# Splitting a sample group's expert pass over two blocks and keeping both halves of the trunk's weights in HBM, in a one-core decoder step

## The chip, the cores and the metric

One core of one Trainium2 chip runs the whole step as one program. The metric is the device time of that program in microseconds (us), the median of several executions. Engines are TensorE (PE in the profile, with PEld for its weight loads), VectorE (DVE), ScalarE (ACT), GpSimd (POOL) and SyncE (SP), which issues most DMAs. A DMA that the program issues from POOL stands in POOL's queue.

## The reference, cut to what matters

One decoder layer over 1024 prompt rows and 64 sample rows, width 1024:

```python
z = rmsnorm(x) @ w_in                       # lru_x | lru_gate | q | k | v | gate_lru | gate_attn
A = rglru(conv(lru_x)) * gelu(lru_gate)     # -> @ w_branch_lru
B = window_attention(q, k, v)               # 128-wide window, ALiBi, sinks -> @ w_branch_attn
merged = sigmoid(gate_lru) * (A @ w_branch_lru) + sigmoid(gate_attn) * (B @ w_branch_attn)
h = x + merged @ w_out
y = h + peer(rmsnorm(h))
# peer: 8 heads x 16 experts for each row, out of 16384, by product keys:
act = gelu(x_row . expert_u[idx]) * g       # 128 experts a row
out = sum(act * expert_v[idx])
```

## The kernel before

The rows pass through the trunk (everything up to `h` and the top-k scores) in three blocks: block 0 has 256 prompt rows and the 64 sample rows, blocks 1 and 2 have 384 prompt rows each. A last stage, `dense`, follows: it walks all 16384 experts for the prompt rows of blocks 0 and 1 and gathers single experts for those of block 2.

**Stages of a block**, in the order in which the code is written (`trunk`): attention; eight steps of gate and attention projection, merged into `mg` (L322 is the eviction); the recurrent branch (`lru`); eight steps of gate and recurrent projection (L337); `w_out` in four column groups (L356); the second norm, whose transposes are L267; and `retrieve`, 16 groups of query projection and top-k.

**Weights.** Matmuls take each float32 operand as a high and a low part (`hi`, `lo`), so that each product is three matmuls (L183 to L185). A weight comes in chunks of 512 KB; there are 84 chunks a block. Block 0 loads a chunk (`wraw`), makes the high part on ACT and the low part on DVE (`split`, L163 and L164), and POOL's queue writes the low part to `lo_d` in HBM (L212). Blocks 1 and 2 load the raw chunk and the low part, and make the high part again on ACT (L208). There are three buffers each for `wraw`, `whi` and `wlo`. The raw chunk is a strided slice of the weight matrix, in runs of 512 or 1024 bytes; `lo_d` lies in runs of 4096 bytes.

**Work behind a block.** What belongs to a block's experts is done while the next block's trunk runs: `behind(b)` is a generator, and `bg(k)` in the trunk advances it by k steps. The tables `PG1` (during block 1) and `PG2` (during block 2) give k for each stage: merge steps, recurrent groups, second merge, `w_out` groups, norm tiles, retrieve groups, q/k/v groups of the attention, score groups. The steps are, in this order:

- `choose(b)`: the top 16 expert pairs of each row, on DVE.
- For block 0 alone, the sample rows' experts: `early_u` gathers 64 slices of `expert_u` (each gather brings 512 KB: 128 rows of 4 KB) by a DMA that POOL issues (L961), and DVE reduces each (L963); `early_v` does the same with `expert_v` (L976, L981) and writes the sample rows' result to `out_y` (L988). Both hold the tile `et`, with three row slots inside it. Two of these go with each step.
- `build_g(b)`: for each group of four rows, one-hot tiles on DVE (`oij`; L939 to L941), four matmuls into a PSUM tile of the tag `tr` (L922), and a copy on ACT into `sg` (L923); a "product" below is one such group. After eight products `sg` goes to HBM (`g_d`, L925). Block 0 has 64 products, block 1 has 96.

**Buffers that are shared.** `et`, `sg` and the attention's keys and values all use the one buffer of the tag `at`: a `sg` can't be written before `et` is done with. The three PSUM tiles of the tag `tr` go round among the products, the norm's transposes and the retrieval, in the order in which the code asks for them.

**Order.** A scheduler puts each engine's instructions into one fixed order when the program is built; an engine then takes them one by one, and waits where the next is not ready.

**Scores** (`scores`): for each block of 128 queries and each key head, four matmuls with 64 contracted rows, two for heads on partitions 0 to 63 and then two for heads on partitions 64 to 127, each pair with its PSUM tile (L460), and four evictions on DVE (L463).

## Time and profile before

| what | value |
|---|---|
| median of 3 runs | 3769.24 us (3755.25 to 3769.95) |
| the profiled execution | 3754.26 us |
| its span, first to last instruction | 3752.5 us |
| PE busy | 3336.7 us, 89% |
| DVE busy | 2882.6 us, 77% |
| POOL busy | 1520.3 us, 41% |
| ACT busy | 1268.9 us, 34% |
| DMA | 1012.37 MB, mean 270 GB/s |

The span begins with the first instruction and ends with the last; times inside it are given from its start. Block 0 ends near 470 us, block 1 near 1235 us, block 2 near 1795 us, and `dense` takes the rest. The profile has a strip of 40 slices (one is 93.8 us) that shows how busy each engine was, and a table of who waited for whom; a wait that an engine spends on something that is not late costs nothing, so a wait counts only where the engine that waits has no other work and the work after it is late too.

### The profile page before, as it was taken

What the parts mean: (1) busy time and instruction counts of PE and PEld (TensorE: products, weight loads), DVE (VectorE), ACT (ScalarE), POOL (GpSimd) and SP (SyncE); (2) the same over time, 40 slices, a digit from 0 to 9 for tenths busy, and PEclk for the clock granted to TensorE, in tenths of its full rate; (3) what the DMA queues carried; (4) which work ended last, traced back from release to release, by engine and by line L of the source; (5) the groups of instructions that cost most, each with busy time, mean ns of one, the idle gap of its engine ahead of it and who ended that gap; (6) DMA issues with size and microseconds to landing.
All of it is one profiled execution on the core that took longest, in us unless ns stands there. A gap on an engine that the chain in (4) does not pass through costs nothing.

```text
span 3752.5 us, 58800 instructions
## 1 busy us (share of the span) xinstructions
PE 3336.7 (89%) x21891; PEld 3211.5 (86%) x21891; DVE 2882.6 (77%) x6803; ACT 1268.9 (34%) x2331; POOL 1520.3 (41%) x1240
## 2 busy tenths in 40 slices
PE   6899999883058989999889999999999999999996
PEld 6798988883058869998779999999999999999996
DVE  5567797984577988867899787777777776777777
ACT  4555454641033455743222222222222222222221
POOL 0011100223400000000367677677767776777774
PEclk8899999987579999999889999999999999999998
DMA  7388856998747627788488989989989888999988
GB/s 230 99 268 282 284 169 194 326 310 309 234 147 266 199 86 245 247 288 280 160 276 300 310 314 317 314 306 320 320 306 312 308 307 305 318 326 313 306 307 284
DMA packets 551327, 1012.37 MB, mean 270 GB/s; under 512 B 39452, under 2 KB 357852, under 8 KB 547936
## 3 DMA queue, kind: packets, MB, share of 16 engines
q1 hardware_dynamic: 409920, 494.75, 40.9%
q0 software_dynamic: 141120, 513.86, 38.5%
q8 instruction: 172, 2.82, 0.3%
q14 instruction: 115, 0.94, 0.1%
HBM read 904.14 MB, written 105.99 MB: 269 GB/s over the span
## 4 chain that ended last, share of the span: by engine, by line
PE 28%; DMA 18%; DVE 13%; issue 8%; POOL 7%; ACT 2%; SPq 0%; POOLq 0%; DVEq 0%; ACTq 0%
DMA row<-in_expert_v,iA 6%; DMA row<-in_expert_u,iA 4%; PE tr L922 3%; DMA et<-in_expert_v,est 3%; PE ou L183 3%; PE ou L184 3%; PE ou L185 3%; PE mm L185 3%; PE mm L183 3%; PE mm L184 3%; PE sc L183 3%; PE sc L184 3%; PE sc L185 3%; POOL row L888 2%; DVE row L890 2%
## 5 line engine op out<-in xcount | busy, mean ns | idle before, releaser
L183 PE MATMUL ou<-ah,vh 128*128 128x384 f32 (+1 forms) x2048 | 634.0, 314 | 42.5 <-ACT ah L163 20.2
L183 PE MATMUL sc<-dx,uh 128*128 128x256 f32 (+1 forms) x2048 | 637.7, 311 | 19.7 <-DVE al L164 10.3
L185 PE MATMUL sc<-dx,ul 128*128 128x256 f32 (+1 forms) x2048 | 635.9, 311 | 1.0 <-POOL ul L164 1.0
L184 PE MATMUL sc<-dx,uh 128*128 128x256 f32 (+1 forms) x2048 | 636.5, 311 | 0.0
L184 PE MATMUL ou<-al,vh 128*128 128x384 f32 (+1 forms) x2048 | 630.5, 310 | 1.9 <-DVE al L164 1.9
L185 PE MATMUL ou<-ah,vl 128*128 128x384 f32 (+1 forms) x2048 | 629.4, 310 | 0.5 <-POOL vl L164 0.5
L164 POOL TENSOR_TENSOR ul<-un,uh 128x1024 fp32r<-128x1024 f32 x128 | 308.2, 2408 | 790.3 <-ACT uh L163 787.4
L902 DVE SCALAR_TENSOR_TENSOR acc<-row,hv,acc 128x1024 f32<-128x1024 f32 x384 | 493.1, 1284 | 127.5 <-DMA row<-in_expert_v,iA 124.3
L890 DVE SCALAR_TENSOR_TENSOR row<-row,xt 128x1024 f32<-128x1024 f32 x384 | 465.0, 1216 | 138.7 <-DMA row<-in_expert_u,iA 136.5
L900 POOL DMA_INDIRECT row<-in_expert_v,iA x384 | 361.6, 942 | 278.6 <-DVE acc L902 202.9
L888 POOL DMA_INDIRECT row<-in_expert_u,iA x384 | 365.8, 953 | 265.5 <-DVE row L890 186.4
L183 PEld LDWEIGHTS ou<-ah,vh 128*128 128x128 f32 x2048 | 385.6, 190 | 59.8 <-DVE dac L1077 27.1
L183 PEld LDWEIGHTS sc<-dx,uh 128*128 128x128 f32 x2048 | 392.5, 192 | 21.4 <-DVE al L164 11.7
L185 PEld LDWEIGHTS sc<-dx,ul 128*128 128x128 f32 x2048 | 391.9, 191 | 1.5 <-POOL ul L164 1.5
L184 PEld LDWEIGHTS sc<-dx,uh 128*128 128x128 f32 x2048 | 392.3, 192 | 0.0
L184 PEld LDWEIGHTS ou<-al,vh 128*128 128x128 f32 x2048 | 388.1, 190 | 3.6 <-DVE al L164 2.7
L185 PEld LDWEIGHTS ou<-ah,vl 128*128 128x128 f32 x2048 | 387.6, 190 | 0.7 <-POOL vl L164 0.7
L922 PE MATMUL tr<-oij 128*128 128x128 f32 x1280 | 169.3, 288 | 202.4 <-ACT sg L923 200.7
L1077 DVE TENSOR_TENSOR dac<-dac,ou 128x384 f32<-128x384 f32 (+1 forms) x672 | 313.8, 481 | 38.2 <-PE ou L185 37.2
L922 PEld LDWEIGHTS tr<-oij 128*128 128x128 f32 x1280 | 164.6, 204 | 206.9 <-ACT sg L923 202.2
L164 POOL TENSOR_TENSOR vl<-vn,vh 128x1024 fp32r<-128x1024 f32 x128 | 309.2, 2420 | 14.6 <-ACT vh L163 12.6
L163 ACT CAST uh<-un 128x1024 fp32r<-128x1024 f32 x128 | 134.4, 1050 | 459.7 <-PE sc L184 360.9
(295 smaller groups left out, 7357.0 us busy)
## 6 DMA issues: line engine op xcount, KB each, us to landing
wlo<-lo_d SPq DMA_DIRECT2D x168, 512.0 KB, 4.9
wraw<-in_w_in SPq DMA_DIRECT2D x132, 512.0 KB, 5.9
un<-in_expert_uT SPq DMA_DIRECT2D x128, 512.0 KB, 5.9
vn<-in_expert_v SPq DMA_DIRECT2D x128, 512.0 KB, 5.8
lo_d<-wlo POOLq DMA_DIRECT2D x84, 512.0 KB, 6.0
g_d<-sg SPq DMA_DIRECT2D x20, 2048.0 KB, 6.9
wraw<-in_peer_w_query SPq DMA_DIRECT2D x48, 512.0 KB, 6.2
gt<-g_d SPq DMA_DIRECT2D x32, 768.0 KB, 10.3
```

Source lines behind the costliest of these rows:

```text
L163: nc.scalar.copy(hi, src)
L164: return (lo_eng or nc.vector).tensor_tensor(lo, src, f32(hi), op=ALU.subtract)
L183: nc.tensor.matmul(ps, lh, rh, start=first and j == 0, stop=False)
L184: nc.tensor.matmul(ps, lh, rl, start=False, stop=False)
L185: nc.tensor.matmul(ps, ll, rh, start=False, stop=last and j == n - 1)
L888: nc.gpsimd.indirect_dma_start(out=row, out_offset=None, in_=i["expert_u"], in_offset=bass.IndirectOffsetOnAxis(ap=ia[:, s:s + 1], axis=0))
L890: nc.vector.scalar_tensor_tensor(row, row, 1.0, xt, op0=ALU.mult, op1=ALU.mult, accum_out=hv[:, s:s + 1])
L900: nc.gpsimd.indirect_dma_start(out=row, out_offset=None, in_=i["expert_v"], in_offset=bass.IndirectOffsetOnAxis(ap=ia[:, s:s + 1], axis=0))
L902: nc.vector.scalar_tensor_tensor(acc, row, hv[:, s:s + 1], acc, op0=ALU.mult, op1=ALU.add)
L922: nc.tensor.matmul(pt[:, x, :], oj[:, x], wi[:, x], start=True, stop=True)
L1077: nc.vector.tensor_tensor(ac[k // 4][:, k % 4, a:b], ac[k // 4][:, k % 4, a:b], ps[:, 0:b - a], op=ALU.add)
```

## The change

- `wsplit`, `load_c` and `load_n` become `weights`: the first block that loads a chunk writes both halves to HBM from POOL's queue (`hi_d` and `lo_d`); the later blocks load both halves and neither load the raw chunk nor copy on ACT.
- `behind`: block 0's generator has `early_u` alone, block 1's generator has `early_v`; one gather goes with a step, no longer two. `early_v` starts in block 2 when the attention has given up the tag `at`.
- `scores`: both PSUM tiles are asked for first, and the four matmuls alternate between the two halves of the partitions; the four evictions follow.
- `PG1` and `PG2` have new numbers.

```diff
-PG1 = (6, 5, 4, 5, 2, 2, 0, 0)
-PG2 = (5, 5, 4, 3, 2, 2, 2, 1)
+PG1 = (5, 5, 4, 5, 2, 2, 0, 0)
+PG2 = (6, 6, 5, 1, 2, 4, 2, 2)
...
-    def wsplit(self, key, hi, lo, raw):
...
-        if use > 1:
-            nc.scalar.copy(hi, raw)
-            nc.sync.dma_start(f32(lo), kept)
-            return
-        self.split(hi, lo, raw)
-        nc.gpsimd.dma_start(kept, f32(lo))
+    def weights(self, src, r0, c0, nk, nc_):
...
+        if first:
+            raw = sp.tile([P, nk, nc_], F32, tag="wraw", name="wraw", bufs=NR)
+            self.wdma = nc.sync.dma_start(raw, src.rearrange("(k p) c -> p k c", p=P)[:, r0:r0 + nk, c0:c0 + nc_])
+            self.split(hi, lo, raw)
+            nc.gpsimd.dma_start(kept[0], f32(hi))
+            nc.gpsimd.dma_start(kept[1], f32(lo))
+        else:
+            nc.sync.dma_start(f32(hi), kept[0])
+            self.wdma = nc.sync.dma_start(f32(lo), kept[1])
...
-            for par in range(2):
...
+            pss = [self.mm().rearrange("p (g s) -> p g s", s=256) for _ in range(2)]
+            for g in range(4):
+                pr = slice(g % 2 * HD, g % 2 * HD + HD)
+                nc.tensor.matmul(pss[g % 2][:, g // 2, 0:S], qT[pr, 2 * j + g // 2, :], kT[pr, j, c0 + b0:c0 + 2 * P], start=True, stop=True)
...
     def behind(self, b):
 
-        early, left = False if b else None, True
+        early, left = None, True
...
-                early = itertools.chain(self.early_u(), self.early_v())
+                early = self.early_v() if b else self.early_u()
...
-            for _ in range(2):
-                if early and next(early, None) is None:
-                    early = False
+            if early and next(early, None) is None:
+                early = False
```

What it does to the order. On DVE in block 1, around the end of `w_out` (`hr` is its result; `et` the sample rows' experts, `oij` the products' tiles), before:

```order
L356 TENSOR_TENSOR hr<-hr,mm 128x256 x2
L963 SCALAR_TENSOR_TENSOR et,eh<-et 128x1024 x7
L966 TENSOR_TENSOR eh<-eh,est 128x64
L979 TENSOR_SCALAR et<-et,eh 128x1024
L981 SCALAR_TENSOR_TENSOR et<-et,eh 128x1024 x63
L986 TENSOR_TENSOR et<-et 64x1024
L987 TENSOR_TENSOR et<-et 64x1024
L940 TENSOR_TENSOR oij<-iof,sT 128x512
```

and after, at the same place:

```order
L349 TENSOR_TENSOR hr<-hr,mm 128x256 x3
L954 SCALAR_TENSOR_TENSOR et,eh<-et 128x1024 x4
L957 TENSOR_TENSOR eh<-eh,est 128x64
L931 TENSOR_TENSOR oij<-iof,sT 128x512
L932 TENSOR_TENSOR oij<-oi,sT 128x512
```

The 63 rows of `early_v`, which stood there in one piece, are gone; the products follow `early_u` at once.

On PE at the end of block 1's `w_out` (`gh` and `gl` are its operands), before and after, with the products that stand ahead of the next norm's transposes:

```order
L185 MATMUL mm<-whi,gl 128x256
L922 MATMUL tr<-oij 128x128 x92
L267 MATMUL tr<-ident,xn 128x128 x4
L183 MATMUL mm<-whi,xh 128x256
```

```order
L186 MATMUL mm<-whi,gl 128x256
L913 MATMUL tr<-oij 128x128 x60
L260 MATMUL tr<-ident,xn 128x128 x4
L184 MATMUL mm<-whi,xh 128x256
```

The run falls from 92 matmuls (23 products) to 60 (15); in both orders 3 products stand earlier in the block.

On PE at the end of block 2's `w_out` (L267 before and L260 after are the transposes of the second norm; L727 those of the recurrent branch's outputs, which stood much earlier before), before and after:

```order
L185 MATMUL mm<-whi,gl 128x256
L922 MATMUL tr<-oij 128x128 x12
L267 MATMUL tr<-ident,xn 128x128 x8
L922 MATMUL tr<-oij 128x128 x8
```

```order
L186 MATMUL mm<-whi,gl 128x256
L913 MATMUL tr<-oij 128x128 x32
L727 MATMUL tr<-ident,st 4x128 x8
L913 MATMUL tr<-oij 128x128 x176
L260 MATMUL tr<-ident,xn 128x128 x8
L913 MATMUL tr<-oij 128x128 x8
```

Before, 80 of block 1's 96 products stand ahead of or at the end of block 2's `w_out`, spread between its matmuls. After, 3 stand early in the block, 6 inside `w_out`, and 52 in the two runs that are shown; 35 are left for the retrieval.

## Rows read from the trace of the kernel before

**Rows 1.** The page's strip of 40 slices: PE's busy tenths, and its granted clock

```profile
PE   6899999883058989999889999999999999999996
PEclk8899999987579999999889999999999999999998
```

**Rows 2.** Busy time by stretch; columns as in the first line

```profile
core 0: us, PE busy (x) PEld busy (x) DVE busy (x) ACT busy (x) POOL busy (x), PEclk, DMA share, GB/s
0.00:186.00 186.00, 145.82 (x987) 128.05 (x988) 104.71 (x344) 88.40 (x246) 10.54 (x23) 0.84 0.51 163
186.00:470.00 284.00, 269.89 (x1865) 259.57 (x1865) 198.42 (x568) 147.92 (x244) 33.01 (x62) 0.99 0.85 279
470.00:606.00 136.00, 129.28 (x807) 104.13 (x806) 111.03 (x447) 77.98 (x209) 1.60 (x3) 1.00 0.45 142
606.00:887.00 281.00, 252.46 (x1424) 240.51 (x1423) 231.77 (x634) 123.64 (x179) 64.65 (x60) 0.94 0.96 321
887.00:1063.00 176.00, 0.00 (x0) 0.00 (x0) 93.10 (x82) 2.37 (x4) 66.22 (x68) 0.51 0.72 229
...
1235.00:1386.00 151.00, 134.97 (x791) 109.14 (x790) 135.61 (x604) 81.72 (x218) 0.00 (x0) 0.95 0.36 114
1386.00:1699.00 313.00, 307.36 (x2041) 301.12 (x2040) 252.71 (x577) 164.70 (x264) 0.00 (x0) 0.99 0.79 261
1699.00:1795.00 96.00, 87.29 (x558) 86.31 (x557) 72.19 (x325) 33.05 (x52) 0.00 (x0) 0.93 0.76 259
1795.00:3752.50 1957.50, 1861.85 (x12408) 1837.38 (x12407) 1545.09 (x2799) 477.88 (x793) 1344.24 (x1024) 0.98 0.88 303
850.00:900.00 50.00, 33.17 (x265) 32.37 (x264) 23.03 (x44) 9.69 (x9) 14.99 (x14) 0.88 1.02 375
```

**Rows 3.** Who waited for whom: us in total, times, longest us

```profile
PE tr L922 <- ACT sg L923: 200.7, 7, 176.9
...
ACT sg L923 <- DMA out_y<-et: 156.2, 1, 156.2
...
PE mm L183 <- ACT Ti L686: 15.1, 9, 3.6
```

**Rows 4.** Tile `et`: duration ns min/median/max, first and last start us

```profile
L963 DVE SCALAR_TENSOR_TENSOR et<-et x64: 1199/1219/1227, 654.7 to 905.1; 128x1024 f32<-128x1024 f32 x64
...
L981 DVE SCALAR_TENSOR_TENSOR et<-et,eh x63: 1283/1284/1341, 913.3 to 1053.1; 128x1024 f32<-128x1024 f32 x63
```

**Rows 5.** Chain that ended last, 1050 to 1101 us: start us, us, what

```profile
1053.10 1.30 DVE et L981
...
1062.89 0.59 ACT sg L923
...
1071.57 6.27 DMA g_d<-sg
1077.93 0.59 ACT sg L923
...
1085.95 6.25 DMA g_d<-sg
1092.30 0.59 ACT sg L923
```

**Rows 6.** PE in order of time, the end of that stretch

```profile
1094.75 6.33 PE L922 MATMUL tr<-oij 128*128 128x128 f32 x48
```

**Rows 7.** DMA issues: number, KB each, median us to landing

```profile
wlo<-lo_d SPq DMA_DIRECT2D x168, 512.0 KB, 4.9
wraw<-in_w_in SPq DMA_DIRECT2D x132, 512.0 KB, 5.9
```

**Rows 8.** One line's instructions: the copy of the high part; columns as in rows 4

```profile
L208 ACT CAST whi<-wraw x168: 1027/1051/1077, 394.7 to 1790.4; 128x1024 fp32r<-128x1024 f32 x168
```

**Rows 9.** Groups by line, the scores' matmuls: busy us, mean ns, idle before

```profile
L460 PE MATMUL mm<-at,qT 64*128 64x256 f32 x224 | 48.1, 409 | 7.5 <-ACT qT L514 3.9 <-DVE sb L463 3.4
```

**Rows 10.** PE's products alone (two records a matmul), up to `w_out`'s end

```profile
1386.00:1699.00 313.00, 79.20 (x639) 77.86 (x640) 0.99 0.79 261
```

More of the change, by code (lines that the diff above doesn't have):

```diff
@@ L86, in __init__ @@
         self.sT_d = self.dr.tile([P, 3, ND], F32, name="sT_d")
+        self.hi_d = self.dr.tile([NCHUNK, P, D], F32, name="hi_d")
         self.lo_d = self.dr.tile([NCHUNK, P, D], F32, name="lo_d")
-        self.chunk, self.uses = {}, {}
+        self.chunk = {}
         self.kcar_d = self.dr.tile([P, NKV, P], F32, name="kcar_d")
@@ L199, in rsqrt @@
             nc.vector.scalar_tensor_tensor(y, t, 1.5, y, op0=ALU.add, op1=ALU.mult)
-    def wsplit(self, key, hi, lo, raw):
-        nc = self.nc
-        m = self.chunk.setdefault(key, len(self.chunk))
-        use = self.uses[key] = self.uses.get(key, 0) + 1
-        kept = self.lo_d[m].rearrange("p (k c) -> p k c", c=raw.shape[2])
-        if use > 1:
-            nc.scalar.copy(hi, raw)
-            nc.sync.dma_start(f32(lo), kept)
-            return
-        self.split(hi, lo, raw)
-        nc.gpsimd.dma_start(kept, f32(lo))
@@ L214, in load_c @@
-    def load_c(self, src, c0):
-        nc, sp = self.nc, self.sp
-        hi = sp.tile([P, KD, P], F32R, tag="whi", name="whi", bufs=NW)
-        lo = sp.tile([P, KD, P], F32R, tag="wlo", name="wlo", bufs=NW)
-        raw = sp.tile([P, KD, P], F32, tag="wraw", name="wraw", bufs=NR)
-        nc.sync.dma_start(raw, src.rearrange("(k p) c -> p k c", p=P)[:, :, c0:c0 + P])
-        self.wsplit((src.name, c0, 0), hi, lo, raw)
-        return hi, lo
-    def load_n(self, src, c0):
-        nc, sp = self.nc, self.sp
-        out = []
-        for h in range(2):
-            hi = sp.tile([P, 4, 256], F32R, tag="whi", name="whi", bufs=NW)
-            lo = sp.tile([P, 4, 256], F32R, tag="wlo", name="wlo", bufs=NW)
-            raw = sp.tile([P, 4, 256], F32, tag="wraw", name="wraw", bufs=NR)
-            self.wdma = nc.sync.dma_start(raw, src.rearrange("(k p) c -> p k c", p=P)[:, 4 * h:4 * h + 4, c0:c0 + 256])
-            self.wsplit((src.name, c0, h), hi, lo, raw)
-            out.append((hi, lo))
-        return out
+    def weights(self, src, r0, c0, nk, nc_):
+        nc, sp = self.nc, self.sp
+        hi = sp.tile([P, nk, nc_], F32R, tag="whi", name="whi", bufs=NW)
+        lo = sp.tile([P, nk, nc_], F32R, tag="wlo", name="wlo", bufs=NW)
+        key = (src.name, r0, c0)
+        first = key not in self.chunk
+        m = self.chunk.setdefault(key, len(self.chunk))
+        kept = [x[m].rearrange("p (k c) -> p k c", c=nc_) for x in (self.hi_d, self.lo_d)]
+        if first:
[7 more added lines that the diff above has]
+            self.wdma = nc.sync.dma_start(f32(lo), kept[1])
+        return hi, lo
@@ L237, in proj_c @@
+    def load_c(self, src, c0):
+        return self.weights(src, 0, c0, KD, P)
+    def load_n(self, src, c0):
+        return [self.weights(src, 4 * h, c0, 4, 256) for h in range(2)]
     def proj_c(self, src, c0, xh, xl, n):
@@ L454, in scores @@
             sb = sp.tile([P, 4, 256], F32, tag="sb", name="sb", bufs=6)
-            for par in range(2):
-                pss = self.mm().rearrange("p (g s) -> p g s", s=256)
-                pr = slice(par * HD, par * HD + HD)
-                for g2 in range(2):
-                    nc.tensor.matmul(pss[:, g2, 0:S], qT[pr, 2 * j + g2, :], kT[pr, j, c0 + b0:c0 + 2 * P], start=True, stop=True)
-                for g2 in range(2):
-                    g = 2 * g2 + par
-                    nc.vector.scalar_tensor_tensor(sb[:, g, 0:S], self.distP[:, b0:], -SLOPES[4 * j + g],
-                                                   pss[:, g2, 0:S], op0=ALU.mult, op1=ALU.add)
+            pss = [self.mm().rearrange("p (g s) -> p g s", s=256) for _ in range(2)]
+            for g in range(4):
+                pr = slice(g % 2 * HD, g % 2 * HD + HD)
+                nc.tensor.matmul(pss[g % 2][:, g // 2, 0:S], qT[pr, 2 * j + g // 2, :], kT[pr, j, c0 + b0:c0 + 2 * P], start=True, stop=True)
+            for g in range(4):
+                nc.vector.scalar_tensor_tensor(sb[:, g, 0:S], self.distP[:, b0:], -SLOPES[4 * j + g],
+                                               pss[g % 2][:, g // 2, 0:S], op0=ALU.mult, op1=ALU.add)
             sm = sp.tile([P, 4, 4], F32, tag="sm", name="sm", bufs=3)
```

## The prediction

> **What bounds the kernel now.** I read the strip first. PE is at 8 or 9 tenths almost everywhere, so TensorE is the bound, with one hole: slices 9 to 11, where it falls to 3, 0 and 5 and its clock to 5 tenths [rows 1]. Next, stretches that I cut at the stages' ends: from 887 to 1063 us PE does nothing at all, just behind block 1's `w_out` [rows 2]. In the other stretches from 186 us on it is busy between 89 and 98%. Then the waits, for the hole's cause: PE waited once for 176.9 us, for ACT's copy into `sg`, and ACT waited 156.2 us in one piece for the DMA that writes the sample rows' result out of `et` [rows 3]. `et` and `sg` share one buffer; the sample rows' gathers run from 654.7 to 1053.1 us on DVE, `early_u` ending at 906.3 and `early_v` after it [rows 4], and only then, at 1062.9, does the first `sg` copy run [rows 5]. So block 1's trunk stands still for a piece of work that isn't its own. Last, the rate at which the products then drain. The first copy of a group of eight comes at 1062.89, 1077.93 and 1092.30, so eight products take 14.7 us, and 6.3 us of that is the write of `g_d`, for which the single buffer waits [rows 5]. The last of the run on PE ends at 1101.1 [rows 6]. The trunk is held from 887 to 1101, 214 us.
>
> All sums are made against the profiled execution, 3754.3 us. The median of the runs shown is 15 us above it, so 15 is added at the end.
>
> **Part 1, the experts in block 1.** `early_v` leaves. `early_u` ends where it did, near 906 us: it has as many rows on DVE, and the order puts its last rows at the end of `w_out` as before. Nothing of `et` is written out there any more, so the first `sg` copy can run at 907. Ahead of the norm stand 3 + 15 products now. With three PSUM tiles, the last of the 18 has to wait for copy 15. That is one group of 14.7 us and then 7 more copies at about 1.1 us (eight take 8.1 us from 1062.9 to the end of the last near 1071, [rows 5]): the trunk goes on at 907 + 22.5 = 929.5 us, 171.5 us earlier than 1101. Eight products more than before are left for the retrieval, at 79.2 / 80 = 0.99 us of PE each [rows 10]: 8 us back. **Part 1: -164 us.** Bounds: -185 if `early_u` ends with `w_out`, -145 if it ends 20 us later. What is late next there is the drain itself.
>
> **Part 2, the experts in block 2.** This is where most of the doubt is, because here the gathers meet the buffer again. `early_v` can start when the attention is over, 1386 us [rows 2]; from 3 us after that. Its pace has two rows: `early_v` alone, beside an idle PE, took (1053.1 - 913.3) / 62 = 2.25 us a row, and `early_u`, beside the same stages of block 1, (905.1 - 654.7) / 63 = 3.97 us [rows 4]. I take the second, since it has the same neighbours: 1389 + 64 x 3.97 = 1643. Then come the fold and the write of the result; before, the `sg` copy began 9.8 us after the last row (1053.1 to 1062.9, [rows 5]). With trunk work in between I take 1650 for the first `sg` copy. It can't be much before 1615: without the products, 79 us of PE work [rows 10], the trunk would reach the end of `w_out` at 1699 - 79 = 1620, and DVE's order has `early_v`'s last rows in `w_out`.
>
> Then 61 products have to go before the second norm's transposes, and the last waits for copy 58: seven groups of 14.7 us and two copies, 105 us. The trunk goes on at 1756 where it did at 1699: 57 us later. There, 35 products are left, before 16: 19 x 0.99 = 17 us more, taking PE as the bound of the retrieval, as its 87 of 96 us say [rows 2]. **Part 2: +74 us.** Bounds: +39 with 1615, +114 with 1690 (4.6 us a row).
>
> **Part 3, the high half in block 0.** Each of the 84 chunks is written once more, 512 KB. In 186 to 470 us POOL issued 62 such writes, 0.53 us each; 62 more find POOL idle. The bytes don't find an idle DMA: that stretch moved 279 GB/s x 284 us = 79.2 MB at a share of 0.85, with PE busy 95% [rows 2]. With 62 x 0.524 = 32.5 MB more it is 111.7 MB. What the DMA can do is bounded by two rows: 375 GB/s at a share of 1.02 between 850 and 900 us, 321 GB/s at 0.96 from 606 to 887 [rows 2]. At the first the stretch takes 298 us, at the second 348. I take 355 GB/s, nearer the row that is full: 315 us. In the first 186 us the share is 0.51 and the 22 writes there are hidden. **Part 3: +31 us**, between +5 and +64. The new write also holds `whi`; with three buffers that is inside this range.
>
> The Trainium skill ("DMA: Bandwidth & Descriptors", section "Where 436 GB/s comes from") puts the limit between HBM and SBUF at about 358 GB/s a core. The 375 of the row is above that; by the page the stretch would take 312 us, +28 instead of +31.
>
> **Part 4, the high half in blocks 1 and 2.** 168 copies of 1.05 us leave ACT [rows 8], which is busy about half of these stretches at most [rows 2]; PE waited for ACT in the trunk mainly at `Ti`, 15.1 us in all blocks [rows 3]. I take -5. The load that replaces the raw chunk lands in 4.9 us, the raw one in 5.9 [rows 7]; PE's waits name no weight load among the longest, so that is -2, and 0 to -10. SP issues as many loads as before, in the same places, so what is queued behind them (`sT`, `est`, `g_d`) keeps its place.
>
> **Part 5, the scores and the tables.** The score matmuls of full width keep PE busy for 48.1 us in all, while their 224 records add up to 224 x 0.409 = 91.6 us [rows 9]: by that row nearly two run at once already, and full pairing would give 48.1 - 45.8 = 2.3 us. I take -3. The other end is -24, half of the 48.1, if the records' lengths overstate the pairing. The Trainium skill ("TensorEngine Tiling (Array Packing)", section "Theoretical Speedup") gives up to 2x for 64 contracted rows; that is the -24, and the row says that most of it is already had. Against it, `PG2` puts 34 steps into block 2's attention, before 22. That attention took 151 us with 22 steps and block 1's 136 us with none [rows 2], 0.7 us a step: +8. **Parts 4 and 5: -2 us**, between -35 and +10.
>
> **Sum**: -164 + 74 + 31 - 2 = -61 us. 3754 - 61 = 3693, and 15 more is **3708 us**. `dense`, 1957 us, has the same instructions and a PE at 95% [rows 2]: unchanged.
>
> **The rivals.**
>
> *The gain is larger.* The writes of part 3 find room (+5), `early_v` keeps up with the trunk (+39), parts 4 and 5 bring -20: -140, **3629 us**. For it: DMA's share in block 0 is 0.85, so 15% is free on the face of it, and the two rows of pace are far apart. Against: DMA at 0.96 to 1.02 in the stage that is most like both [rows 2].
>
> *It comes out even.* Part 3 at +64 and part 2 at +114: +12, **3781 us**. For it: both are DMA-bound stretches, and a DMA that is full in one is likely to be so in the other. In block 2 the stage 1386 to 1699 has a share of 0.79 already, without gathers [rows 2].
>
> *Slower, by the pace of `early_v` in block 2.* The mechanism: each row waits for its gather, three are in flight, and all 61 products wait for the last row. At 6 us a row the first `sg` copy runs at 1389 + 384 + 10 = 1783, the trunk goes on at 1889, part 2 is +207 and the sum +72: **3841 us**. It decides from 4.9 us a row on (1389 + 64 x 4.9 + 10 = 1713, part 2 at +137, the sum +2), and from 5.2 it is over 0.5% slower. For it: block 2 now moves both weight halves, gathers and the sample's output in one stage. Against: block 1 did the like at 3.97 us.
>
> *The change doesn't do what it says*: block 1's trunk waits as long as before, because `early_u` runs later with one gather a step instead of two. Then part 1 is nothing and the sum +103: **3872 us**. Against: the order has `early_u` at the same stages as before, and only four of its rows behind `w_out`.
>
> **How the numbers follow.** Forecast 57%, larger gain 18%, even 13%, slower by the pace 9%, no removal 3%. The forecast's own range is 3660 to 3750. The range for 8 in 10 leaves out the two slower cases and the lower half of the larger gain: 3635 to 3785 us. A measurement of this kernel tells about 0.5%, 19 us, from no change: faster by more than that 75%, within it 13%, slower 12%.
>
> **What would show it.** Right: no slice of PE near zero at 9 to 11; the wait of PE for the `sg` copy split into a short one behind block 1's `w_out` (near 20 us) and a drain behind block 2's, where PE is under half busy for about 100 us while `sg` copies come in groups of eight every 14.7 us; block 0 some 30 us longer, with a DMA share near 1 from 186 us on; `early_v`'s rows in block 2 near 4 us apart. Wrong: a block 0 as long as before, `early_v` ending well before `w_out`, or the products draining at another rate than 14.7 us for eight. The forecast falls if the two long runs of products in block 2 don't hold the trunk.

## The result, and the profile after

The changed kernel takes **3737.4 us** (median), the kernel before 3761.9 beside it: a ratio of 0.9936, 95% interval 0.9921 to 0.9951, some 24 us or 0.6% faster. One of its 16 runs, at a granted clock of 0.555, took 5484 us and is not in the ratio. The forecast was 3708. The profiled execution has a span of 3725.4 us, 27.1 below the 3752.5 of before, and this is how they part. A block runs from the last matmul of one retrieval (PE, `tr<-skT,qr`) to that of the next; the loop is `dense`, from its first score matmul to the end. By these marks the three blocks of before end at 515, 1273 and 1813 us; the round 470, 1235 and 1795 used ahead cut off the last groups of each retrieval.

| us | before | after | difference | forecast |
|---|---|---|---|---|
| block 0 | 515.0 | 541.0 | +26.0 | +31 |
| block 1 | 757.9 | 593.5 | -164.4 | -164 |
| block 2 | 540.0 | 640.8 | +100.8 | +74 |
| between, and the loop | 9.8 + 1929.7 | 9.5 + 1940.5 | +10.5 | 0 |
| parts 4 and 5, over all blocks | | | in the rows above | -2 |

Block 1 in pieces: from its start to the second norm's first transpose 585.9 to 408.3; from there to the end of the retrieval 172.0 to 185.2. Block 2 in pieces: attention (to the first `mg` eviction) 113.2 to 116.4; from there to the end of `w_out` 313.2 to 281.2; from there to the second norm's first transpose 1.7 to 98.0; from there to the end of the retrieval 112.0 to 145.3.

The strip after, for [rows 1]: the hole of slices 9 to 11 (counted from 0) is gone, and two shallow dips, to 7 tenths, stand in slices 16 and 19.

```profile
PE   6888899988898998788799999999999999999996
...
PEclk8899999999998999888899999999999999999998
```

Busy time by stretch, for [rows 2], cut at the stages after (columns in the first line):

```profile
core 0: us, PE busy (x) PEld busy (x) DVE busy (x) ACT busy (x) POOL busy (x), PEclk, DMA share, GB/s
187.00:511.00 324.00, 287.90 (x1925) 271.17 (x1926) 209.16 (x627) 146.99 (x244) 68.14 (x128) 0.98 0.99 354
187.00:541.00 354.00, 316.06 (x2135) 297.09 (x2136) 237.74 (x799) 150.89 (x254) 68.68 (x129) 0.98 0.95 341
641.00:915.00 274.00, 247.35 (x1417) 235.49 (x1415) 234.16 (x640) 71.15 (x125) 70.16 (x63) 0.97 0.90 333
915.00:949.00 34.00, 16.64 (x118) 16.45 (x119) 23.31 (x44) 9.35 (x18) 0.94 (x1) 0.75 0.50 194
...
1251.00:1532.00 281.00, 246.91 (x1450) 234.94 (x1448) 202.42 (x363) 69.73 (x123) 73.88 (x61) 0.96 0.91 337
1532.00:1630.00 98.00, 63.24 (x408) 61.08 (x409) 87.84 (x201) 34.08 (x67) 0.00 (x0) 0.76 0.52 200
1630.00:1730.00 100.00, 99.20 (x665) 98.22 (x664) 71.59 (x230) 26.22 (x51) 0.00 (x0) 1.00 0.61 217
1730.00:1776.00 46.00, 29.61 (x123) 21.83 (x121) 41.71 (x233) 4.97 (x9) 0.00 (x0) 0.68 0.28 109
...
1785.00:3725.00 1940.00, 1845.66 (x12328) 1821.36 (x12328) 1519.10 (x2634) 476.20 (x789) 1346.52 (x1024) 0.98 0.88 304
```

The trunk of block 1 waits 34 us behind `w_out` where it waited 214; that of block 2 waits 98, with PE 63 of them busy and a mean granted clock of 0.76. DMA is near full from 187 to 541 us (share 0.95, and 0.99 up to 511; before 0.85 [rows 2]). In 1730 to 1776 PE is the waiter and VectorE (41.7 of 46 us) the bound.

Who PE waited for, over the whole run, for [rows 3]: the wait for the `sg` copies is 55 us where it was 201, its longest piece 12.7 where it was 176.9, and one that was small before (4.1 us at the end of block 2's retrieval) is that for VectorE's top-k (`s`), all but little of it in those last 46 us.

```profile
PE tr L913 <- ACT sg L914: 55.4, 10, 12.7
...
PE mm L184 <- ACT Ti L677: 17.9, 12, 2.7
PE tr L757 <- DVE s L762: 15.6, 25, 1.4
```

The tile of the gathers, for [rows 4]: `early_u` in block 1 ends at 926 (906 before), 3.7 us a row; `early_v` in block 2 goes from 1253.7 to 1501.9, (1501.9 - 1253.7) / 62 = 4.00 us a row.

```profile
L954 DVE SCALAR_TENSOR_TENSOR et<-et x64: 1176/1216/1226, 692.2 to 925.4; 128x1024 f32<-128x1024 f32 x64
...
L972 DVE SCALAR_TENSOR_TENSOR et<-et,eh x63: 1267/1280/1290, 1253.7 to 1501.9; 128x1024 f32<-128x1024 f32 x63
```

And the chain in block 1, for [rows 5]: the first `sg` copy follows the last row within 1.5 us, since nothing of `et` is written out there any more.

```profile
925.36 1.25 DVE et L954 x2
...
926.89 0.48 ACT sg L914
...
934.45 6.25 DMA g_d<-sg
...
940.79 0.59 ACT sg L914
```

### The profile page after: what moved, and what is told of

The parts are those of the page before. It is cut to its first block, busy times and chain, and to the rows that moved or that the text cites. A ratio compares the mean times of both kernels' runs of the same rounds, so it can differ in the third digit from the quotient of the medians.

```text
span 3725.4 us, 58732 instructions
## 1 busy us (share of the span) xinstructions
PE 3367.4 (90%) x21891; PEld 3218.6 (86%) x21891; DVE 2875.5 (77%) x6803; ACT 1108.2 (30%) x2162; POOL 1585.4 (43%) x1324
## 4 chain that ended last, share of the span: by engine, by line
PE 38%; DMA 21%; DVE 19%; issue 11%; POOL 7%; ACT 3%; POOLq 0%; SPq 0%; DVEq 0%; ACTq 0%
DMA row<-in_expert_v,iA 7%; PE mm L184 5%; PE mm L186 5%; PE mm L185 5%; DMA row<-in_expert_u,iA 4%; PE ou L184 3%; PE ou L185 3%; PE ou L186 3%; PE tr L913 3%; PE sc L184 3%; PE sc L185 3%; PE sc L186 3%; POOL row L879 2%; DVE acc L893 2%; DVE row L881 2%
## 5 line engine op out<-in xcount | busy, mean ns | idle before, releaser
L184 PE MATMUL ou<-ah,vh 128*128 128x256 f32 (+1 forms) x2048 | 633.3, 314 | 55.7 <-DVE dac L1067 30.9
L185 PE MATMUL ou<-al,vh 128*128 128x256 f32 (+1 forms) x2048 | 629.9, 310 | 2.3 <-DVE al L165 2.3
L186 PE MATMUL ou<-ah,vl 128*128 128x256 f32 (+1 forms) x2048 | 628.6, 310 | 0.9 <-POOL vl L165 0.9
L967 POOL DMA_INDIRECT et<-in_expert_v,est x64 | 77.9, 1217 | 488.4 <-PE pso L489 323.8
L184 PE MATMUL mm<-xh,whi 128*128 128x384 f32 (+1 forms) x768 | 258.7, 337 | 24.4 <-ACT Ti L677 17.9
L164 ACT CAST uh<-un 128x1024 fp32r<-128x1024 f32 x128 | 134.4, 1050 | 470.6 <-PE sc L185 342.8
```

The source lines that it names most:

```text
L164: nc.scalar.copy(hi, src)
L184: nc.tensor.matmul(ps, lh, rh, start=first and j == 0, stop=False)
L185: nc.tensor.matmul(ps, lh, rl, start=False, stop=False)
L186: nc.tensor.matmul(ps, ll, rh, start=False, stop=last and j == n - 1)
L967: nc.gpsimd.indirect_dma_start(out=row(s), out_offset=None, in_=self.i["expert_v"], in_offset=bass.IndirectOffsetOnAxis(ap=self.es[:, 0, s ...
```

## The experiments

Fifteen runs. Their times, and the stages of their profiles (us; ratio to before with its interval; e5 and e11 are one profiled execution each):

| run | ratio | block 0 | block 1 | block 2 | loop |
|---|---|---|---|---|---|
| before | | 515.0 | 757.9 | 540.0 | 1929.7 |
| after | 0.9936 (0.9921 to 0.9951) | 541.0 | 593.5 | 640.8 | 1940.5 |
| e1 split only | 0.9950 (0.9929 to 0.9971) | 504.2 | 594.9 | 677.9 | 1943.2 |
| e2 weights only | 1.0109 (1.0081 to 1.0137) | 550.7 | 754.7 | 541.7 | 1940.3 |
| e3 own rows | 0.9828 (0.9801 to 0.9854) | 548.2 | 559.6 | 610.9 | 1952.8 |
| e4 light products | 0.9951 (0.9933 to 0.9970) | 550.2 | 591.1 | 638.1 | 1945.0 |
| e5 before again | | 513.8 | 756.9 | 541.3 | 1936.3 |
| e6 even retrieval | 0.9989 (0.9972 to 1.0006) | 548.8 | 597.2 | 636.0 | 1968.8 |
| e7 ACT copies | 1.0003 (0.9989 to 1.0018) | 551.8 | 597.7 | 637.0 | 1957.4 |
| e8 own rows, half pace | 0.9802 (0.9779 to 0.9825) | 543.0 | 565.4 | 610.0 | 1958.2 |
| e9 rows off VectorE | 0.9825 (0.9802 to 0.9847) | 548.2 | 576.7 | 626.8 | 1937.9 |
| e10 the same, half pace | 0.9810 (0.9787 to 0.9833) | 555.5 | 562.8 | 633.2 | 1941.1 |
| e11 light products again | | 552.2 | 584.4 | 640.3 | 1954.7 |
| e12 e8, other loop order | 0.9767 (0.9743 to 0.9792) | 547.1 | 563.2 | 607.5 | 1954.6 |
| e13 e6, other loop order | 0.9929 (0.9904 to 0.9953) | 544.0 | 596.4 | 633.7 | 1945.7 |
| e14 e6 again | 0.9977 (0.9958 to 0.9996) | 551.5 | 596.0 | 639.2 | 1973.6 |
| e15 after again | 0.9933 (0.9910 to 0.9956) | 553.1 | 596.4 | 640.1 | 1943.7 |

### e1 and e2: each part alone

e1 is the kernel before with the new `behind` and the new tables; e2 is the changed kernel with the old `behind` and the old tables:

```diff
-        early, left = False if b else None, True
+        early, left = None, True
...
-                early = itertools.chain(self.early_u(), self.early_v())
+                early = self.early_v() if b else self.early_u()
...
-            for _ in range(2):
-                if early and next(early, None) is None:
-                    early = False
+            if early and next(early, None) is None:
+                early = False
```

> The kernel before with the sample rows' experts divided between blocks 1 and 2 and the new tables of steps, but with the old weights (raw chunk and low half, the copy on ACT) and the old order of the score products. Theory: the split by itself is worth what the two traces show of blocks 1 and 2, -164 and +100 us, and block 0 ends as before (last matmul of its retrieval near 515 us): 3754 - 64 = 3690, a ratio of 0.983, about 28 us better than the changed kernel. Rival 1: the 26 us that block 0 lost have nothing to do with the second write, so they stay here: retrieval of block 0 ending near 540, ratio 0.990. Rival 2: the saved ACT copies were worth more than thought, and here block 1 and block 2 lose by 168 copies of 1.05 us on ACT: ratio 0.995 or more.

> The changed kernel with the experts of the sample rows all in block 1 again and with the old tables of steps: the second half of the weights kept by block 0, and the new order of the score products, alone. Theory: block 0 ends 26 us later (retrieval near 541), the hole in block 1 is back (trunk held until about 1127), little else: 3754 + 26 - 5 = 3775, a ratio of 1.006. Rival: what block 0 loses comes back in blocks 1 and 2, because ACT is rid of 168 copies and the loads carry the final data: ratio 0.995 to 1.000.

Alone, the split gains 0.5% and the weights lose 1.1%; together they gain 0.6%. The parts don't add up: -19 and +41 us make +22, and the two together are -24. The profiles say where the difference lies: 39 us of it in block 2, since e1 takes 37 more there than after, and 13 in the loop, which is longer in e1 and in e2 than before and so is counted twice. e1's theory fell and so did its rival 1 (block 0 ends at 504); the size is that of rival 2, and e7 asks whether its cause holds. e2 came out dearer than its theory had it, by block 0 (+36) and the loop (+11).

The price of the second write is clear: from the first `mg` eviction of block 0 to the end of its retrieval it takes 331 to 333 us in the three profiles without it (before, e1, e5) and 357 to 370, mean 364, in the fourteen with it: **+32 us**. What it buys depends on the stage. In e2, block 2 has no gathers, and nothing comes back (541.7 for 540.0). In block 1 of e1 there are gathers beside raw weights, at a DMA share of 0.97, and still the block is as long as after (594.9, 593.5): the rows of `early_u` come 3.84 us apart in place of 3.70, but begin 9 us sooner in the block. In block 2, e1 has gathers beside the raw weights and takes 677.9 us, 37 more than after. Of these, 26 lie between the attention's end and the first `sg` copy (292 us, after 266): 20 since `early_v` takes (1497.2 - 1229.4) / 62 = 4.32 us a row in place of 4.00, and some 7 between its last row and that copy. Another 11 are in the attention, where the DMA share is 0.22 (after 0.25), so that the weights' traffic doesn't explain them; e1 has the old order of the score products there as well, and no run tells the two apart. In e1 the two stretches named, then its rows:

```profile
1099.00:1226.00 127.00, 105.71 (x458) 74.44 (x459) 119.29 (x432) 62.64 (x183) 3.17 (x3) 0.83 0.22 71
596.00:870.00 274.00, 245.63 (x1420) 233.66 (x1418) 230.59 (x634) 120.68 (x177) 66.15 (x60) 0.98 0.97 328
```

```profile
L963 DVE SCALAR_TENSOR_TENSOR et<-et x64: 1168/1218/1226, 646.2 to 888.0; 128x1024 f32<-128x1024 f32 x64
...
L981 DVE SCALAR_TENSOR_TENSOR et<-et,eh x63: 1231/1279/1289, 1229.4 to 1497.2; 128x1024 f32<-128x1024 f32 x63
```

The stretch up to `w_out`'s end in block 2 of e1 (columns as above), its packets, and those of the same stretch after:

```profile
1226.00:1507.00 281.00, 244.21 (x1399) 232.79 (x1398) 186.57 (x338) 118.45 (x168) 72.70 (x61) 0.96 0.97 327
```

```profile
DMA packets 67991, 92.02 MB, mean 327 GB/s; under 512 B 2784, under 2 KB 52704, under 8 KB 67717
```

```profile
DMA packets 26205, 94.78 MB, mean 337 GB/s; under 512 B 3217, under 2 KB 3985, under 8 KB 25803
```

In e1 DMA is at 0.97 for less traffic, after it is at 0.91 for more: the raw chunk is a slice of a wider matrix and comes in 45,824 packets of 512 bytes, 30 ns each in the trace, 17.4 bytes a ns. The kept half after comes in 4 KB packets, 177 ns each, 23.2 bytes a ns, and so do the gathered rows in e1. The Trainium skill ("DMA: Bandwidth & Descriptors", section "Specifications") gives 512 bytes as the least that moves at line rate; here they move at three quarters of what 4 KB does, and the trace decides.

### e7: was it ACT?

```diff
             self.wdma = nc.sync.dma_start(f32(lo), kept[1])
+            raw = sp.tile([P, nk, nc_], F32, tag="wraw", name="wraw", bufs=NR)
+            nc.scalar.copy(raw, f32(hi))
```

> The changed kernel with 168 needless copies on ACT: behind each reload of a weight chunk's two halves in blocks 1 and 2 ACT copies the high half into one of the raw buffers, which nobody reads. Same DMA packets as in the changed kernel, as much work on ACT as with the old weights. The kernel with the split alone lost 37 us against it in block 2. Theory A (that was the raw chunks' DMA: 45,824 packets of 512 bytes at 30 ns in 1226 to 1507 us, 17.4 bytes a ns where packets of 4 KB carry 23): no difference here, block 2 near 641 us, ratio 0.992 to 0.995. Theory B (it was ACT, which did the copies and the products' sg copies): block 2 some 30 us longer, ratio 1.000 to 1.004.

With as much ACT work as the old weights made, block 2 takes 637.0 us, no more than after, and `early_v` 3.86 us a row: the 26 us were not ACT's. The packets remain as their cause by exclusion; no run changed the packets alone. The ratio is not theory A's but lies in theory B's range (1.0003). Of the profiles' difference of 27 us, 11 are in block 0, where the copies don't run (after's 541.0 is the lowest of the kernels with the second write; the same kernel in e15 has 553.1), and 17 in the loop, where they don't either. The loop is taken up below.

### e3, e8: is it the shared buffer that holds the trunk?

The gathered rows move into the three raw-weight buffers, the row input or sum into an `s4` tile, and `behind` runs rows and products side by side. e8 takes a row at every second step, with flatter tables:

```diff
+            row = self.sp.tile([P, D], F32, tag="wraw", name="erow", bufs=NR)
...
+        for _ in itertools.chain(self.choose(b), self.build_g(b)):
             if early is None and self.es is not None and self.at_free:
                 early = self.early_v() if b else self.early_u()
...
             if early and next(early, None) is None:
                 early = False
             yield True
...
+        while early and next(early, None) is not None:
             yield True
```

> The changed kernel, but the gathered expert rows lie in the three 4 KB buffers of the raw weights, which stand empty after block 0, and the rows' input or sum in one of the four-buffer 4 KB tiles; so the buffer of the products' copies is never held by the gathers, and the products run beside the gathers, step by step, as they did in block 2 of the kernel before. All else, the tables too, as in the changed kernel. Theory (the shared buffer is what holds the trunk): the drains behind w_out go, in block 1 about 20 us and in block 2 about 98, and the 30 us more in block 2's retrieval; some of it comes back as 61 products' PE time in the trunk and a fuller DMA: 3727 - 90 = 3640, ratio 0.968 to 0.975. Rival (DMA and DVE are full anyway, the gathers at 4 us a row set the pace wherever the products stand): trunk of block 2 stretched by the products, w_out of block 2 ending 60 to 100 us later than in the changed kernel, ratio 0.990 to 1.000.

> The kernel with own buffers for the gathered rows, with a row at every second step instead of every step, and tables near those of before (block 1: 5, 4, 4, 3, 2, 2; block 2 as before: 5, 5, 4, 3, 2, 2, 2, 1), so that rows and products spread over the whole trunk and a few products into the retrieval. With a row at every step VectorE was busy 185 of 200 us from 1300 to 1500 and PE 163. Theory A (that crowding on VectorE held the trunk): block 2 shorter by 20 to 60 us than the 611 of the kernel with own buffers, ratio 0.968 to 0.978. Theory B (the rows' DMA work costs the trunk the same wherever it stands): block 2 within 10 us of 611, ratio 0.981 to 0.986. Rival C: rows that come later hold VectorE in w_out and the norm, where it has slack now: longer, above 0.986.

Theory and rival of e3 were half right. The wait behind block 2's `w_out` is gone (1.7 us for 98.0), and the retrieval, with no products left in it, takes 90.4 us for 145.3. But the stretch from the attention to `w_out`'s end grows from 281 to 383 us, and the attention from 116 to 136: the products stand there again (79 us of PE before [rows 10]), and VectorE is crowded. In e3, then e8:

```profile
1300.00:1500.00 200.00, 163.38 (x926) 152.52 (x926) 184.61 (x303) 84.76 (x149) 77.41 (x46) 0.89 0.82 299
```

```profile
1290.00:1350.00 60.00, 37.18 (x202) 35.70 (x201) 57.77 (x95) 9.23 (x19) 24.06 (x18) 0.78 0.78 277
```

VectorE is the third column of busy time: 185 of 200 us, and 58 of 60. What is left of the gain is 30 us in block 2 and 34 in block 1. Half the pace changed block 2 by 1 us (610.0), as theory B of e8 had it; the tables changed with the pace, so the two are not told apart. The ratio, 0.9802, fell between the two theories. That VectorE's load is what holds the trunk here is likely but not shown; e9 and e10 were to test it.

### e9, e10: the rows off VectorE

In block 2 ACT scales a row and GpSimd adds it; e10 is e8 with this edit alone:

```diff
...
-                nc.vector.scalar_tensor_tensor(acc, row, self.eh[:, s:s + 1], acc, op0=ALU.mult, op1=ALU.add)
+            nc.scalar.activation(row if s else acc, row, AF.Copy, scale=self.eh[:, s:s + 1])
+            if s:
+                nc.gpsimd.tensor_tensor(acc, acc, row, op=ALU.add)
```

> The kernel with own buffers for the gathered rows, a row at every step, tables 4, 4, 4, 3, 2, 2 in block 1 and those of before in block 2 (5, 5, 4, 3, 2, 2, 2, 1); in block 2 the sum over the rows of expert_v is taken off VectorE: ACT scales a row, GpSimd adds it to the sum. That takes 64 x 1.27 = 81 us from VectorE, which was busy 97 percent of 1290 to 1350 us while PE was at 62 percent. Theory A (VectorE holds block 2's trunk when rows, choice and products share it): block 2 falls from 610 us to 550 to 585, ratio 0.966 to 0.976. Theory B (the gathers' DMA work holds it: 32 MB more beside 82 MB): block 2 stays at 595 to 615, ratio 0.978 to 0.984. Rival C: GpSimd's adds take VectorE's port, and its instructions grow longer by as much as it saves: as B, with VectorE's products well over 0.69 us.

> The same, with a row at every second step (block 1: 5, 4, 4, 3, 2, 2). Theory A: block 2 within 10 us of the kernel with a row at every step, since VectorE no longer minds where the rows stand. Theory B (DMA): shorter by 10 to 30 us than that, since the gathers are spread over the whole trunk.

Block 2 is longer, 627 and 633 us for 610, though VectorE lost 81 us of work: by its mechanism this is rival C, and by its size more than any of the theories had. VectorE's busy time in block 2 rose, in e8 and then in e10 (columns as above):

```profile
1108.00:1718.00 610.00, 534.48 (x3280) 495.22 (x3279) 521.44 (x1456) 199.08 (x442) 101.19 (x61) 0.93 0.68 251
```

```profile
1118.00:1752.00 634.00, 546.96 (x3282) 503.79 (x3280) 558.93 (x1397) 262.25 (x504) 258.50 (x124) 0.92 0.66 242
```

So the instructions that stayed on it grew by some 118 us (558.9 - 521.4 + 81). VectorE was not relieved, and so neither run says whether its load holds the trunk. VectorE's instructions (duration min/median/max in ns, first and last start) in block 2 of e8, then of e9, and GpSimd's add in e9:

```profile
L931 DVE TENSOR_TENSOR oij<-iof,sT x89: 671/683/739, 1281.2 to 1602.1; 128x512 f32<-128x512 f32 x89
...
L813 DVE TENSOR_TENSOR eq<-ce,bf x16: 977/982/993, 1242.0 to 1324.0; 128x800 f32<-128x800 f32 x16
L815 DVE TENSOR_REDUCE ev<-eq x16: 972/976/987, 1243.1 to 1325.0; 128x16 f32<-128x800 f32 x16
```

```profile
L931 DVE TENSOR_TENSOR oij<-iof,sT x87: 676/680/3536, 1300.5 to 1638.4; 128x512 f32<-128x512 f32 x87
...
L813 DVE TENSOR_TENSOR eq<-ce,bf x16: 977/1508/3189, 1245.6 to 1318.3; 128x800 f32<-128x800 f32 x16
L815 DVE TENSOR_REDUCE ev<-eq x16: 966/986/986, 1246.6 to 1320.4; 128x16 f32<-128x800 f32 x16
...
L643 DVE COPY st<-xr x8: 154/170/2374, 1321.3 to 1414.5; 128x3 f32<-128x3 f32 x8
...
L969 POOL TENSOR_TENSOR ex<-ex,erow x62: 2342/2410/10653, 1230.2 to 1603.5; 128x1024 f32<-128x1024 f32 x62
```

Half of the `oij` instructions are as short as ever, and some are longer by about one GpSimd add (3536 - 680 = 2856 beside 2410). `eq` and `oij` read two tiles of SBUF; the reduction, which reads one, is untouched (986 at most). One form with a single input was drawn out too: the small copy into `st`, up to 2374 ns (351 at most in e8). The Trainium skill ("SBUF — State Buffer", section "Who interferes with whom") divides them in this way: a VectorE instruction with two SBUF inputs contends with a GpSimd instruction that reads SBUF, through a pair of ports that is an exclusive lock; one with at most one SBUF input, outside the two-port modes, does not. The trace agrees for `oij`, `eq` and the reduction; whether the copy ran in a two-port mode no view here shows.

### e4, e6, e11: the drain and the retrieval

e4 (and e11, which is the same kernel once more) makes one of four rows of each product on VectorE and leaves out the other three, so that its products are wrong; e6 changes one number of the table:

```diff
-PG2 = (6, 6, 5, 1, 2, 4, 2, 2)
+PG2 = (6, 6, 5, 1, 2, 2, 2, 2)
```

> The changed kernel with one of the four rows of each one-hot product made on VectorE, and used four times by the matmuls; the other three are left out, so that g_d holds the wrong products. VectorE's cost of a product falls from 1.78 us (0.42 + 0.68 + 0.68) to about 0.8; matmuls, the copies into sg and the writes of g_d are as before. Theory A (the drain behind w_out is bound by the single copy buffer: eight copies and the write of g_d, 8.1 + 6.3 us): the drain stays at 14.5 to 15.5 us for eight products, and the norm of block 2 starts as late as now, near 1630. Theory B (it is bound by VectorE, 8 x 1.78 = 14.3 us): it falls below 12 us for eight. For the end of block 2's retrieval, which VectorE's top-k work shares with the last 35 products: under A and B alike the stretch from the norm to the retrieval's last matmul shrinks from 145 us by up to 35, if VectorE bounds it as the trace says; it stays at 145 if PE does, as the prediction had it.

> The changed kernel with two steps instead of four behind each of the 16 groups of block 2's retrieval; the tables ahead of it as they are, so the same products stand ahead of the norm and 35 in the retrieval. Theory A (the retrieval's first half is bound by PE, with four products a group, and its last six or seven groups by VectorE's top-k, 1.6 us for each of three tiles; evened out, both work side by side): from the norm to the last matmul of the retrieval it takes 115 to 130 us instead of 145, ratio to before about 0.987 to 0.990. Theory B (VectorE's whole work there, 77 us of top-k and 35 x 1.78 us of products, is the bound however it is dealt out): it stays within 5 us of 145, ratio 0.992 to 0.995.

The drain behind `w_out` doesn't care about VectorE: from the first `sg` copy of the first group to that of the eighth, eight products take (1633.7 - 1527.5) / 7 = 15.2 us in e4, 15.5 after and 14.7 in e15. So it is the chain of eight products with their copies and one write of `g_d`, as [rows 5] had it. In the retrieval neither change does what its theory A wanted: 141.6 us with light products, 136.6 with two products a group, after 145.3. In e4 the stretch splits as after:

```profile
1638.00:1738.00 100.00, 99.66 (x673) 98.70 (x671) 55.34 (x236) 26.52 (x53) 0.00 (x0) 1.00 0.63 233
1738.00:1780.00 42.00, 26.57 (x114) 19.25 (x112) 37.18 (x225) 4.43 (x9) 0.00 (x0) 0.69 0.21 82
```

While the products last PE has no gap (99.7 of 100 us) and VectorE has many; when all but the last few are done, 28 of the 48 top-k steps are left, VectorE is nearly full and PE waits for it. The two bounds come one behind the other: after, PE's busy time in the two stretches is 128.8 us and VectorE's 113.3, and neither alone would make the 145. So lightening VectorE's share of the products buys little, 3.7 us. With the tables' four numbers side by side, no product in the retrieval gives 90.4 us (e3), 16 give 112.0 (before), 35 give 145.3 at four a group and 136.6 at two: 1.35, 1.57 and 1.32 us for one product, where the sum had 0.99. Dealing them out evenly takes back 9 of the 33 us by which the retrieval grew; that a product costs 1.3 us even so, with PE busy 123 of 137 us in e6, is not explained further.

### e5, e11 to e15: the loop

e5 is before once more, e15 after, e14 is e6. e12 and e13 are e8 and e6 with 16 and 64 small copies on VectorE behind the retrieval, which leave the blocks' order as it is and lead the scheduler to deal out the loop in another order:

```diff
             self.dense_x()
+            for _ in range(16):
+                self.nc.vector.tensor_copy(self.eh, self.est[:, 1])
```

> The kernel before once more, for a second profile of it. The stretch from the first score matmul of the experts' loop to the end took 1929.7 us in the first profile of before, and 1940 to 1953 us in the five kernels since. Theory A (it is spread between executions): it takes 1938 to 1950 us here. Theory B (the changed kernels run that loop in another order of VectorE's instructions, and pay for it): it takes 1927 to 1933 us again.

> To be read beside the changed kernel and the one with two steps a group: one of four rows of each one-hot product made on VectorE (the others are left out, so that g_d holds wrong products). A second execution of the light kernel with four steps a group, whose experts' loop has the same order of instructions as the kernel with the needless ACT copies (1945.0 and 1957.4 us there). Theory A (the loop's time differs between executions by what is not in the order): 1938 to 1965 us. Theory B (the order alone sets it): 1950 to 1957. The norm to the retrieval's last matmul: 141.6 us again, within 3.

> The kernel with own buffers for the gathered rows and a row at every second step, with 16 small copies on VectorE (128 x 64 elements, into a tile nobody reads again) issued behind block 2's retrieval. They leave the three blocks' instructions in their order and shift the planner's clock, so that it deals out the instructions of the experts' loop in another order, close to that of the changed kernel. Theory A (the order in which the loop's instructions stand on PE and VectorE sets its time, and an edit ahead of the loop changes it by chance): the loop takes 1938 to 1944 us, as in the five kernels with about this order (1937.9, 1940.3, 1940.5, 1941.1, 1943.2), instead of 1958, and the ratio falls from 0.980 to 0.973 to 0.978. Theory B (the loop's time depends on what the blocks before left behind, or on the execution): it stays at 1950 to 1965 us, ratio 0.979 to 0.982.

> The changed kernel with two steps instead of four behind each group of block 2's retrieval, with 64 small copies on VectorE in the same place, which bring the experts' loop near the order of the changed kernel. Theory A (order): the loop takes 1938 to 1946 us instead of 1968.8, block 2 about 636 us, ratio 0.990 to 0.993 instead of 0.999. Theory B (not the order): the loop stays at 1955 to 1975 us, ratio 0.996 to 1.001.

> The changed kernel with two steps instead of four behind each group of block 2's retrieval, once more, as the neighbour of the one with the other order of the loop. Theory A: the loop takes 1960 to 1975 us, ratio 0.997 to 1.001 again. Theory B: it may come anywhere from 1938 to 1970.

> The changed kernel once more, beside the others. Theory A: the loop takes 1938 to 1944 us, ratio 0.992 to 0.996 again. Theory B: it may come anywhere from 1930 to 1970 us.

The loop's instructions are the same in all kernels; their order is not. Position by position, 5681 of some 12,330 instructions on PE stand elsewhere after than before. By order, the loop takes:

- in that of before (before, e5): 1929.7 and 1936.3 us;
- in that of after (after, e15, and e1, e2 and e10 with under 600 positions changed): 1940.5, 1943.7, 1943.2, 1940.3, 1941.1; a little farther from it (1,100 to 1,350 positions) e9 1937.9, e13 1945.7 and e12 1954.6;
- in that of e4, e7 and e11, the same in all three: 1945.0, 1957.4, 1954.7;
- in that of e6 and e14, and e3 950 positions from it: 1968.8, 1973.6, 1952.8. e8 has one of its own, 1958.2.

The clearest pair is e14 and e13, with the same instructions in the blocks: 1973.6 to 1945.7, and the ratio from 0.998 to 0.993. The profile of e14 is a long execution of that kernel (3772 us); by the medians of all runs the pair differs by 22 us (3758.9, 3736.5). PE's waits in the loop, with VectorE's longest wait for ACT, in e14 and then in e13:

```profile
PE ou L184 <- DVE dac L1067: 36.6, 33, 4.6
PE ou L184 <- ACT ah L164: 35.2, 27, 2.7
```

```profile
PE ou L184 <- DVE dac L1067: 27.9, 32, 4.3
PE ou L184 <- ACT ah L164: 19.2, 20, 3.5
```

```profile
DVE al L165 <- ACT ah L164: 72.8, 72, 4.9
```

```profile
DVE al L165 <- ACT ah L164: 47.2, 58, 4.0
```

So the order is a cause, worth some 22 us here. That the changed kernel's 9 us (1942 in the mean for 1933) are of the same kind is likely, with two profiles of before and seven near after's order (e12 left out) that don't overlap, but no run gave after's blocks the loop order of before. The order is not the whole: the same one gave 1945.0 and 1957.4, and the medians of those two kernels, e4 and e7, lie 25 us apart (3739.5, 3764.0) though their blocks differ by 7 us at most. So e7's time stays unexplained, e11 fits both of its theories, e5 fell between its two, and e12 took 1954.6, theory B's loop time, with theory A's ratio. e13, e14 and e15 came as their theory A had them. What in an order makes it slow, and why e12 kept its loop time, stays open. e12 is the fastest kernel of the study, **3680.6 us, ratio 0.9767** (0.9743 to 0.9792); its gain over e8 (0.9802) is within the two intervals.

## Why the prediction was wrong

The direction held; the size did not: -24 us of a forecast -61.

- **Part 1 came out right, in part by luck.** -164 was forecast, -164.4 came. But the trunk went on 178 us sooner in the block (585.9 to 408.3), not 171.5, and the eight products more in the retrieval cost 13 us (172.0 to 185.2), not 8. The two misses cancel. In the trace the trunk went on at 949 where it had stood until 1101; `early_u` ended 20 us later than assumed, since block 0 had shifted all by 26.
- **Part 3 was right.** +31 was forecast, +26 came in the first profile and +32 in the mean of fourteen. Its stretch ran at a DMA share of 0.99 and 354 GB/s up to 511 us, where 355 was taken. Its lower bound, +5, had no row: the fuller of its two rows gives 298 us, +14.
- **Part 2 holds the step that failed.** +74 was forecast and +101 came. Two of its numbers held: the rows' pace (3.97 forecast, 4.00 measured) and the first `sg` copy (264 us behind the attention forecast, 266 measured). The hold at the norm was +57 in the sum and +64 net in the trace (98.0 - 1.7, less the 32 by which `w_out` came sooner), with 15.5 us for eight products, not 14.7; in e15, the same kernel, it is 14.7 and +62. The larger miss is **the price of a product left in the retrieval**, and e15 shows it too (145.1 us): 19 more at 0.99 us were +17 "taking PE as the bound" (19 x 0.99 is 18.8); it came to +33. The 0.99 was read where products stand spread through the trunk; in the retrieval of before they already cost 1.35 each. In [rows 2] PE and VectorE were both near full there, 87 and 72 of 96 us, and the sum took the second's work to fit beside the first. Bunched at four a group the products made PE the bound first and VectorE afterwards, in 1730 to 1776 us (e4); dealt out at two a group they still cost 1.32 (e6). The bunching is shown, the rest of the price stays open. The same price is what part 1 missed in block 1.
- **That the pace held rests on part 4.** The sum took the pace from block 1 of before, with raw weights, and gave the kept high half -5 and -2 us. e1 shows that with raw weights block 2's rows go at 4.32 us and its first `sg` copy comes 26 us later; e7 shows that ACT had no part in it. So the right pace, too, is two errors that cancel. The term that was mis-sized is the load of the high half: worth nothing where DMA has room (e2), 1 us in block 1 and 26 us in block 2, both with DMA near full. By landing times [rows 7], 4.9 beside 5.9 us, about a sixth of the raw chunk's DMA time could have been read as at stake.
- **Part 5.** The scores' alternation was taken as -3. Their group after reads as [rows 9] did, 48.3 us busy for 48.1:

```profile
L452 PE MATMUL mm<-at,qT 64*128 64x256 f32 x224 | 48.3, 424 | 6.1 <-DVE sb L454 3.6 <-ACT qT L505 2.3
```

  Neither the -3 nor the -24, the "up to 2x" of the Trainium skill ("TensorEngine Tiling (Array Packing)", section "Theoretical Speedup"), is there. Block 2's attention grew by 3.2 us, not 8; the two stretches that the 8 was read from hold the ends of the retrievals as well.
- **"`dense` is unchanged" was wrong** by 11 us. It has the same instructions, but the scheduler orders the whole program, and an edit ahead of the loop reorders it (e13, e14); that this is the cause of the 11 is likely, not shown.

The sum of the misses: -5 in block 0, +27 in block 2, +11 in the loop, and the -2 of parts 4 and 5 that didn't show make 34 or 35, from -61 to -27. By size the result lies midway between the forecast and the rival "it comes out even", whose mechanism was not the one that decided: the second write didn't reach +64, and part 2 came near its +114 without the slower pace behind it. Of what would show it, the groups of eight, the pace of `early_v` and the longer block 0 came as written; the wait in block 1 was 34 us, not near 20, and PE was busy 63 of 98 us in the drain, not under half.

## What to carry to other kernels

Price a piece of work by the two engines that it uses, stage by stage: work that fits beside one bound can make another engine the last, and bunching it puts the two bounds one behind the other. Two parts of a change can hang on each other: keeping weights in whole 4 KB rows cost 32 us and gave back 26 in one stage with gathers, 1 in another and nothing where there were none, so neither part alone told what it was worth in the other's company. A forecast that comes out right term by term can still hide errors that cancel. And where a scheduler orders a whole program, a stretch that the diff doesn't touch can still move by a per cent.

## What was not expected of the hardware

512-byte packets moved 17.4 bytes a ns and the gathers' 4 KB packets 23.2, in the same stretch (e1). GpSimd adds of 2.4 us drew single VectorE instructions with two SBUF inputs out from 0.68 to 3.5 us (e9), some 118 us in all over block 2 (e10), and left a one-input reduction alone, though not a small copy. And two kernels with the same instructions in the loop, in two orders, ran 22 us apart (e13, e14).
